# Delta rule's preparation: four buffers for the decay factors, masks in the preparation's own pool, gating weights in the weight ring, and the last triangular inverses behind the first head's loads

## The chip, the cores and the metric

The kernel runs on one core of a Trainium2 chip. The metric is the device time of one execution in microseconds (us), as the median of several runs. The names of the engines in the profile are: PE the matrix engine (PEld its weight loads), DVE the vector engine, ACT the scalar engine, POOL the general engine, SP the engine whose queue issues nearly all transfers.

## The reference, cut to what matters

The program computes a hybrid layer (a mixer of delta rule and differential attention, then experts) and after it a second block (a state space branch, sparse attention, a feed-forward part). The change lies in the mixer of the first block. Its delta rule, chunk by chunk:

```
a_mat = eye + b * (k k^T) * dec_strict          # one 64x64 triangle a chunk and head
sol   = triangular_solve(a_mat, [b*exp(G)*k, b*v])
def step(s, xs):                                # in order over the chunks, both directions
    u = ub - w @ s
    o = qd @ s + aqk @ u
    return gl * s + kd^T @ u, o
```

and its differential attention, for 4 heads and blocks of 128 queries, with 256 context tokens ahead of 1024 own keys:

```
s = einsum('bqhid,bkhid->bhiqk', qi, k)         # two maps i for each head
p = softmax(s)
a = p[:, :, 0] - lam * p[:, :, 1]
o = einsum('bhqk,bkhe->bqhe', a, v)
```

Both outputs, normed and gated, go side by side through `w_out`.

## The kernel before, in words

Everything here happens in `stage_mixer`, in chunks of 128 tokens: 10 tiles (tiles 0 and 1 are the context), 4 heads, two directions d.

First come the projections. After the convolutions of q, k and v, `gdn_prep` treats one tile: it transposes and norms k, q and v, makes k k^T (`kks`) and q k^T (`qks`), and for each direction the decays: the matmul of `g` with `tri` gives the sums of log decays in PSUM, one matmul with `mask` (L423) adds -2^60 where the triangle is empty, ACT takes exponents into a tile `e1` (shown as `e`), DVE multiplies it by `qks` (L428, stored to DRAM as `Qk`) or by `kks` (L433, stored as `Ad`). A latent tile takes four `e1` tiles: two a direction. ACT can write an `e1` only when the store that reads the buffer's last content has ended.

`gdn_invert` inverts the 32x32 diagonal blocks of `Ad` of a group of tiles, all blocks at once, a partition each: it loads them (`ia`, L452), negates into `im` (L454, L455), and goes over 31 columns with a multiply (L462) and an add (L464) on DVE, then a transposing copy (L466) and stores to `XT`. There are three groups: tiles 0 and 1; 2, 3, 8, 9; 4 to 7. The code writes each group's inverse behind the preparation of the next group; the last one stands alone, ahead of `sr.close()`.

Then follow, in the order of the code, the projections of differential attention (`da_proj_qk`), the load of head 0 (`da_load`: `dalq`, `dalk`, `da_v`, split on ACT and DVE into `da_qh`, `da_ql` L680, `da_ka` L683), and the gate projection (`gate_proj`).

The second half runs the recurrence and the attention side by side. `gdn_merge` builds the whole inverses (`mX`, `mT`) of two tiles from the 32x32 blocks (`mc<-XT`), `Ad` (`mB`) and k (`mk`); `gdn_step` makes `u` (L575), the new state `S` and outputs. There are 10 steps of two (one a direction); step 4 is the first that needs tiles of the third group. `da_unit` is one of 32 units (4 heads by 8 query blocks): six score matmul pairs (`sc`), six minima on DVE (`dst`, L713), six exponents on ACT (`E`, L714), three multiplies on POOL (L728), three combinations on DVE (L729), ten transposes (`atp`) and the product with v. Its output is `o_sb` (L744).

A scheduler fixes every engine's order when the program is built. It takes what the code writes first as more urgent, moves instructions past each other where tiles and engines are free, and so interleaves projections, preparation, recurrence and units. On the chip every engine and queue then works in its fixed order, and SP issues transfers one after the other. Pools own memory: a pool opened after another was closed may lie on the closed one's bytes, and then waits until its last reader is done. In the kernel before, `gi` (the inverse's tiles `ia`, `im`, `ix`) is closed by `sr.close()`, and the pools `hd0` and `dal` of head 0, on the right side, come behind it.

Of the kernel before, what the change touches and what calls it, by code (L numbers as in the profile page):

```python
# [10 lines left out]
F32 = mybir.dt.float32  # L11
F32R = mybir.dt.float32r
# [4 lines left out]
ALU = mybir.AluOpType  # L17
# [231 lines left out]
def gdn_scalars(K, gs, wk, ps):  # L249

    nc, I = K.nc, K.I
    sb = wk.tile([16, 4], F32, name="sb", bufs=1)
    nc.vector.memset(sb[:, 0:1], -1.0)
    nc.vector.memset(sb[0:8, 0:1], 1.0)
    nc.vector.memset(sb[:, 1:3], 0.0)
    nc.sync.dma_start(sb[0:8, 1:2], I["dt_bias"].rearrange("a d h -> (a d h)")[:, None])
    nc.sync.dma_start(sb[0:8, 2:3], I["a_log"].rearrange("a d h -> (a d h)")[:, None])
    nc.scalar.activation(sb[:, 3:4], sb[:, 2:3], AF.Exp)
    z = wk.tile([16, NT], F32, name="abz", tag="cvraw", bufs=1)
    e = wk.tile([16, NT], F32, name="abe", tag="cva")  # L260
    wr = gs.tile([128, 8, 16], F32, name="abw", bufs=1)
    nc.sync.dma_start(wr, I["w_in"][0].rearrange("(k p) n -> p k n", p=128)[:, :, 3584:3600])
    w = gs.tile([128, 8, 48], F32R, name="abh", bufs=1)
    for c in (0, 16):
        nc.scalar.activation(w[:, :, c:c + 16], wr, AF.Copy)
    nc.vector.tensor_sub(w[:, :, 32:48], wr, w[:, :, 0:16].bitcast(F32))
    for c0, n in CHUNKS:
        q = ps.tile([128, 512], F32, name="pj")
        for k in range(8):
            K.mm(q[0:48, :n], w[:, k], K.hh[:, k, c0:c0 + n], k == 0, False)  # L270
            K.mm(q[0:16, :n], w[:, k, 0:16], K.hl[:, k, c0:c0 + n], False, k == 7)
        nc.scalar.activation(e[:, c0:c0 + n], q[32:48, :n], AF.Copy)
        nc.vector.tensor_add(z[:, c0:c0 + n], q[0:16, :n], e[:, c0:c0 + n])
    nc.vector.tensor_scalar(z, z, sb[:, 0:1], sb[:, 1:2], op0=ALU.mult, op1=ALU.add)
    nc.scalar.activation(e, z, AF.Abs)
    nc.scalar.activation(e, e, AF.Exp, scale=-1.0)
    nc.scalar.activation(e, e, AF.Ln, bias=1.0)
    nc.vector.tensor_scalar(z, z, 0.0, None, op0=ALU.max)
    nc.vector.tensor_add(z, z, e)
    nc.vector.tensor_scalar(z, z, sb[:, 3:4], -1.0, op0=ALU.mult, op1=ALU.mult)  # L280
    g = gs.tile([128, 10, 16], F32, name="g_tok")
    K.g = g
    tp = K.ga.tile([128, 512], F32, name="ga")
    for t in range(10):
        nc.tensor.transpose(tp[:, t * 16:(t + 1) * 16], z[:, t * 128:(t + 1) * 128], K.ident[:16, :16])
    nc.vector.tensor_copy(g, tp[:, :160].rearrange("p (t c) -> p t c", c=16))
    K.tri = []
    for d in range(2):
        m = gs.tile([128, 128], F32, name=f"tri{d}")
        nc.gpsimd.memset(m, 1.0)  # L290
        sg = 1 if d == 0 else -1
        nc.gpsimd.affine_select(out=m, in_=m, pattern=[[sg, 128]], compare_op=ALU.is_ge, fill=0.0,
                                base=0, channel_multiplier=-sg)
        K.tri.append(m)
    cp = K.ga.tile([128, 512], F32, name="ga")
    G = cp[:, 0:80].rearrange("p (t c) -> p t c", c=8)
    for d in range(2):
        K.mm(cp[:, 40 * d:40 * d + 40], K.tri[d], g[:, :, 4 * d:4 * d + 4], True, True)
    K.mm(cp[:, 80:160], K.ones, g[:, :, 0:8], True, True)
    G = gs.tile([128, 2, 10, 4], F32, name="G")  # L300
    GL = gs.tile([128, 2, 10, 4], F32, name="GL")
    nc.vector.tensor_copy(G, cp[:, 0:80].rearrange("p (d t c) -> p d t c", d=2, c=4))
    nc.vector.tensor_copy(GL, cp[:, 80:160].rearrange("p (t d c) -> p d t c", d=2, c=4))
    K.nG = gs.tile([128, 2, 10, 4], F32, name="nG")
    nc.vector.tensor_scalar(K.nG, G, -1.0, None, op0=ALU.mult)
    K.nGb = gs.tile([128, 2, 10, 4], F32, name="nGb")
    for d in range(2):
        nc.vector.tensor_add(K.nGb[:, d], K.nG[:, d], g[:, :, 8 + 4 * d:12 + 4 * d])
    K.rq = gs.tile([128, 8, 4], F32, name="rq")
    K.identr = gs.tile([128, 128], F32R, name="identr")  # L310
    nc.vector.tensor_copy(K.identr, K.ident)
    K.mask = []
    for d in range(2):
        m = gs.tile([128, 4, 128], F32R, name=f"mask{d}")
        nc.vector.tensor_scalar(m, K.tri[d].unsqueeze(1).to_broadcast([128, 4, 128]), 2.0 ** 60, -2.0 ** 60,
                                op0=ALU.mult, op1=ALU.add)
        K.mask.append(m.rearrange("p h i -> p (h i)"))
    kds = gs.tile([128, 2, 10, 4], F32, name="kds")
    nc.vector.tensor_sub(kds, GL, G)
    nc.scalar.activation(kds, kds, AF.Exp)  # L320
    nc.scalar.activation(G, G, AF.Exp)
    nc.scalar.activation(GL, GL, AF.Exp)
    beta = gs.tile([128, 2, 10, 4], F32, name="beta")
    for d in range(2):
        nc.scalar.activation(beta[:, d], g[:, :, 8 + 4 * d:12 + 4 * d], AF.Exp)
    K.eG, K.glb, K.kds, K.beta = G, GL, kds, beta
# [41 lines left out]
def gdn_prep(K, wk, t):  # L368
    nc = K.nc
# [44 lines left out]
    for d in range(2):  # L414
        gr = K.ga.tile([128, 4, 128], F32, name="ga")
        for h in range(4):
            K.mm(gr[:, h], K.g[:, t, 4 * d + h:4 * d + h + 1].to_broadcast([128, 128]), K.tri[d], h == 0, True)
        if lat:
            eg = wk.tile([128, 4, 128], F32, name="eg", bufs=2)
            nc.scalar.activation(eg, gr, AF.Exp)  # L420
            nc.vector.tensor_mul(eg, eg, qt)
            nc.sync.dma_start(K.Qd[d, t - 2], eg)
        K.mm(gr.rearrange("p h i -> p (h i)"), K.identr, K.mask[d], False, True)  # L423
        e1 = wk.tile([128, 4, 128], F32, name="e1", bufs=2)
        if lat:
            for h in range(4):
                nc.scalar.activation(e1[:, h], gr[:, h], AF.Exp, bias=K.nG[:, d, t, h:h + 1])
            nc.vector.tensor_mul(e1, e1, qks)  # L428
            nc.sync.dma_start(K.Qk[d, t - 2], e1)
            e1 = wk.tile([128, 4, 128], F32, name="e1", bufs=2)  # L430
        for h in range(4):
            nc.scalar.activation(e1[:, h], gr[:, h], AF.Exp, bias=K.nGb[:, d, t, h:h + 1])
        nc.vector.tensor_mul(e1, e1, kks)  # L433
        nc.sync.dma_start(K.Ad[d, t].rearrange("h j i -> j h i"), e1)
# [229 lines left out]
def da_load(K, hd, lp, h):  # L664
    nc = K.nc
    q = lp.tile([128, L], F32, name="dalq")
    k = lp.tile([128, NT], F32, name="dalk")
    nc.sync.dma_start(q, K.qrd[h])
    nc.sync.dma_start(k, K.krd[h])
    v = hd.tile([128, 10, 128], F32, name="da_v")  # L670
    nc.sync.dma_start(v, K.vd[:, h * 128:(h + 1) * 128].rearrange("(t p) e -> p t e", p=128))
    lo, hi = slice(0, 64), slice(64, 128)
    Q, KA = [], []
    sub = (nc.gpsimd if h else nc.vector).tensor_sub
    for i, (a, b) in enumerate(((lo, hi), (hi, lo))):
        qh = hd.tile([128, L], F32R, name=f"da_qh{i}")
        ql = hd.tile([128, L], F32R, name=f"da_ql{i}")
        for c in (a, b):
            nc.scalar.activation(qh[c], q[a], AF.Copy, scale=-0.125)
            nc.vector.scalar_tensor_tensor(ql[c], q[a], -0.125, qh[a].bitcast(F32), op0=ALU.mult, op1=ALU.subtract)  # L680
        ka = hd.tile([128, NT], F32R, name=f"da_ka{i}")
        nc.scalar.activation(ka[a], k[a], AF.Copy)
        sub(ka[b], k[a], ka[a].bitcast(F32))  # L683
        Q.append((qh, ql))
        KA.append(ka)
    return Q, KA, v
# [106 lines left out]
def stage_mixer(K, cst, dr):  # L793

    nc, I, tc = K.nc, K.I, K.tc
# [21 lines left out]
    with ExitStack() as s0:  # L817
        gs = K.pool(s0, "gs", 1)
        sp = s0.enter_context(ExitStack())
        K.ga = K.pool(sp, "gap", GAB, PSUM)  # L820
        sr = s0.enter_context(ExitStack())
        with ExitStack() as s1:
# [6 lines left out]
            with ExitStack() as s2:  # L829
                wk = K.pool(s2, "cvw", 2)  # L830
                da_lambda(K, wk, ps)
                gdn_scalars(K, gs, wk, ps)
                w = wcols(K, win, 2048)
# [6 lines left out]
                gdn_conv(K, wk, ps, wcols(K, win, 1536), 0, K.qTd)  # L840
                gdn_conv(K, wk, ps, wcols(K, win, 2560), 2, K.vTd)
            dp = K.pool(s1, "dpw", 2)
            gi = K.pool(sr, "gi", 1)
            wk = K.pool(sr, "gw", 1, side="right")
            ahead = []
            for ts in ((0, 1), (2, 3, 8, 9), (4, 5, 6, 7)):
                for t in ts:
# [1 line left out]
                if ahead:  # L849
                    gdn_invert(K, gi, ahead.pop())  # L850
                ahead.append(ts)
            gdn_invert(K, gi, ahead.pop())
            sr.close()
            hdp = [K.pool(s0, "hd0", 1, side="right")]
            lp = K.pool(s0, "dal", 1, side="right")
# [10 lines left out]
                da_proj_qk(K, wk, ps, w, h, K.krd, True)  # L866
            w = wcols(K, win, 3072)
            hd = da_load(K, hdp[0], lp, 0)
            gate_proj(K, wk, ps, w)
        with ExitStack() as s1:  # L870
            sp.close()
# [1647 lines left out]
```

## Time and profile before

| | us |
|---|---|
| median of 3 runs | 3219.5 (3216.84 to 3223.82) |
| profiled execution, own time | 3220.71 |
| its span from first to last instruction | 3219.0 |
| its mean granted clock of PE | 0.952 of full |
| busy in the span: PE / DVE / ACT / POOL | 2899.8 / 2399.3 / 1635.2 / 654.3 |
| last projection matmul of the mixer starts | 527.41 |
| first score matmul of the first attention unit | 636.5 |
| last transfer of the mixer's outputs issued | 1042.12 |

All positions are us from the start of the profiled span. The stretch between the last three rows is where this change works; from 1042 on, the order of the program is not touched. "Busy" is the time in which at least one instruction runs on the engine, so overlapping ones are not counted twice.

### The profile page before, as it was taken

The numbers are of one execution on the slowest core, as the hardware profiler recorded it, in microseconds if no ns is written. First come the engines' busy times: TensorE is split into PE (matmuls) and PEld (weight loads), VectorE is DVE, ScalarE is ACT, GpSimd is POOL, SyncE is SP. The second block draws the span as 40 slices with busy tenths as digits, with TensorE's granted clock in tenths as the row PEclk, the third lists the DMA queues.
The fourth block names the chain that finished last, engine by engine and source line by source line (L and its number), as shares of the span: only waits on it lengthen the run. The fifth ranks groups of instructions, "written<-read, shape, count | busy, mean of one in ns | idle before, by whom it ended". The sixth has DMA issues, their size and how long they took to land.

```text
span 3219.0 us, 45364 instructions
## 1 busy us (share of the span) xinstructions
PE 2899.8 (90%) x15797; PEld 2390.6 (74%) x15797; DVE 2399.3 (75%) x4935; ACT 1635.2 (51%) x3127; POOL 654.3 (20%) x606
## 2 busy tenths in 40 slices
PE   6899996688897959999999699998798999999999
PEld 3678885677786748887777577776686788888787
DVE  4387676879887499999988599986566686555675
ACT  3333454246676228887777477663443243333343
POOL 1000111245545521110100424432225000000000
PEclk8999998789899979999999899999899999999999
DMA  6466655643224449999997223224575323333732
GB/s 224 114 209 183 192 180 169 177 118 111 71 77 140 176 181 379 384 398 373 364 367 265 84 63 92 66 64 136 147 237 183 118 72 105 111 110 100 291 112 102
DMA packets 366211, 567.04 MB, mean 176 GB/s; under 512 B 72581, under 2 KB 207646, under 8 KB 365982
## 3 DMA queue, kind: packets, MB, share of 16 engines
q1 hardware_dynamic: 361374, 547.37, 50.1%
q0 software_dynamic: 4608, 16.78, 2.2%
q8 instruction: 124, 2.03, 0.3%
q14 instruction: 105, 0.86, 0.1%
HBM read 446.12 MB, written 117.95 MB: 175 GB/s over the span
## 4 chain that ended last, share of the span: by engine, by line
PE 65%; DVE 18%; DMA 7%; issue 4%; ACT 4%; POOL 1%; SPq 1%; DVEq 0%; ACTq 0%; POOLq 0%
PE pj L57 37%; PE pu L57 5%; PE pg L57 5%; PE py L57 4%; PE ga L57 3%; PE lg L57 2%; PE atp L57 2%; DVE E L729 1%; DVE bjv L1778 1%; DVE dst L713 1%; DVE wl L1229 1%; PE sc L57 1%; DMA s5wo<-s5o 1%; DMA wmod<-in_w_mod_dram 1%; PE tp L1252 1%
## 5 line engine op out<-in xcount | busy, mean ns | idle before, releaser
L1229 DVE TENSOR_TENSOR wl<-wraw,wh 128x1024 fp32r<-128x1024 f32 x384 | 446.7, 1219 | 10.6 <-ACT wh L1228 10.3
L1228 ACT ACTIVATE wh<-wraw 128x1024 fp32r<-128x1024 f32 x384 | 391.7, 1060 | 79.6 <-PE pu L57 36.9
L57 PE MATMUL pj<-hh,wh 128*128 128x512 f32 (+1 forms) x768 | 296.7, 386 | 10.7 <-ACT uo L1928 7.7
L57 PE MATMUL pj<-hl,wh 128*128 128x512 f32 (+1 forms) x768 | 292.4, 381 | 0.0
L57 PE MATMUL pj<-hh,wl 128*128 128x512 f32 (+1 forms) x768 | 292.1, 382 | 0.0
L57 PE MATMUL pj<-wh,hh 128*128 128x512 f32 (+1 forms) x400 | 161.0, 403 | 18.7 <-DVE g L2018 8.5
L57 PEld LDWEIGHTS pj<-hh,wh 128*128 128x128 f32 x768 | 145.4, 189 | 42.4 <-ACT uo L1928 10.9
L57 PEld LDWEIGHTS pj<-hh,wl 128*128 128x128 f32 x768 | 144.8, 189 | 30.1 <-issue 3.9
L57 PEld LDWEIGHTS pj<-hl,wh 128*128 128x128 f32 x768 | 145.5, 189 | 26.9 <-issue 2.9
L57 PE MATMUL pj<-wh,hl 128*128 128x512 f32 (+1 forms) x400 | 159.2, 399 | 1.6 <-DVE hl L214 1.5
L57 PE MATMUL pj<-wl,hh 128*128 128x512 f32 (+1 forms) x400 | 159.9, 400 | 0.0
L714 ACT ACTIVATE E<-sc,dst 128x512 f32<-128x512 f32 (+1 forms) x192 | 117.4, 616 | 71.7 <-DVE dst L713 66.2
L75 ACT ACTIVATE wh<-wraw 128x1024 fp32r<-128x1024 f32 (+2 forms) x88 | 88.8, 1015 | 91.2 <-DMA wraw<-in_w_in_dram 36.6
L76 POOL TENSOR_TENSOR wl<-wraw,wh 128x1024 fp32r<-128x1024 f32 (+1 forms) x44 | 100.2, 2281 | 138.1 <-ACT wh L75 137.9
L713 DVE TENSOR_REDUCE dst<-sc 128x1 f32<-128x512 f32 (+1 forms) x192 | 108.7, 594 | 10.5 <-PE sc L57 9.4
L57 PE MATMUL pu<-wl,xh 128*128 128x512 f32 x256 | 101.6, 397 | 11.3 <-DVE wl L1229 11.0
L728 POOL TENSOR_TENSOR E<-E,dst 128x512 f32<-128x512 f32 (+1 forms) x96 | 97.5, 1044 | 65.6 <-DVE dst L725 37.2
L57 PE MATMUL sc<-da_ka,da_qh 128*128 128x512 f32 (+1 forms) x192 | 81.3, 427 | 30.8 <-ACT E L714 30.8
L1775 ACT ACTIVATE bja<-isc,bca 128x384 bf16<-128x384 f32 (+2 forms) x96 | 79.4, 827 | 51.6 <-DVE bca L1793 24.8
L57 PEld LDWEIGHTS pj<-wh,hh 128*128 128x128 f32 x400 | 77.9, 195 | 35.9 <-DVE g L2018 8.9
L1292 POOL DMA_INDIRECT xacc<-ye,ix x16 | 37.1, 2318 | 324.9 <-DVE ye L1291 239.2
L57 PE MATMUL pg<-wl,xh 128*128 128x512 f32 x256 | 102.6, 401 | 0.2 <-DVE wl L1229 0.2
(825 smaller groups left out, 8513.4 us busy)
## 6 DMA issues: line engine op xcount, KB each, us to landing
wraw<-in_w_gate_dram SPq DMA_DIRECT2D x64, 1024.0 KB
wraw<-in_w_up_dram SPq DMA_DIRECT2D x64, 1024.0 KB
wraw<-in_w_down_dram SPq DMA_DIRECT2D x64, 1024.0 KB
wraw<-in_w_in_dram SPq DMA_DIRECT2D x52, 512.0 KB
raw<-hsd SPq DMA_DIRECT2D x38, 512.0 KB
mw<-in_w_mod_dram SPq DMA_DIRECT2D x32, 512.0 KB
raw<-in_w_ffn_gate_dram SPq DMA_DIRECT2D x22, 512.0 KB
raw<-in_w_ffn_up_dram SPq DMA_DIRECT2D x22, 512.0 KB
```

The lines of the kernel that those rows point to most:

```text
L57: self.nc.tensor.matmul(out, lhsT, rhs, start=start, stop=stop, skip_group_check=True)
L75: nc.scalar.activation(h, raw, AF.Copy)
L76: self.sub(l, raw, h.bitcast(F32))
L713: nc.vector.tensor_reduce(mn[:, i, j:j + 1], p[:, :n], axis=AX.X, op=ALU.min)
L714: nc.scalar.activation(e[:, c0:c0 + n], p[:, :n], AF.Exp, bias=mn[:, i, j:j + 1], scale=-1.0, accum_out=ls[:, i, j:j + 1])
L728: nc.gpsimd.tensor_mul(e1, e1, sc[:, 1, j:j + 1].to_broadcast([128, n]))
L729: nc.vector.scalar_tensor_tensor(e0, e0, sc[:, 0, j:j + 1], e1, op0=ALU.mult, op1=ALU.add)
L1228: nc.scalar.activation(h, raw[:, k], AF.Copy)
L1229: nc.vector.tensor_sub(l, raw[:, k], h.bitcast(F32))
L1252: nc.tensor.transpose(tp[:, k], src[:, (k0 + k) * 128:(k0 + k + 1) * 128], K.ident)
L1292: nc.gpsimd.indirect_dma_start(out=K.xacc, out_offset=bass.IndirectOffsetOnAxis(ap=idx[e][:, :1], axis=0), in_=ye, in_offset=None, compute ...
L1775: self.K.nc.scalar.activation(jk[:, :self.n], self.x, AF.Sign, bias=cand, scale=-1.0, accum_out=cnt)
```

## The change: what it does

1. `e1` gets four buffers in the place of two.
2. The two `mask` tiles are no longer made in the long-lived pool `gs` but in the preparation's own pool `gw`, ahead of the first `gdn_prep`.
3. The gating weights `abw` and `abh` take slots of the weight ring's pools (`wraw`, `wh`) in the place of places of their own in `gs`.
4. `gi` is opened in the scope `s1`, which lives until the projections are through, so `sr.close()` no longer closes it.
5. The last `gdn_invert` (tiles 4 to 7) is written behind head 0's `da_load` and ahead of `gate_proj`.

```diff
--- before.py
+++ after.py
@@ -258,9 +258,9 @@
     nc.scalar.activation(sb[:, 3:4], sb[:, 2:3], AF.Exp)
     z = wk.tile([16, NT], F32, name="abz", tag="cvraw", bufs=1)
     e = wk.tile([16, NT], F32, name="abe", tag="cva")
-    wr = gs.tile([128, 8, 16], F32, name="abw", bufs=1)
+    wr = K.wraw.tile([128, 8, 16], F32, name="abw", tag="wraw")
     nc.sync.dma_start(wr, I["w_in"][0].rearrange("(k p) n -> p k n", p=128)[:, :, 3584:3600])
-    w = gs.tile([128, 8, 48], F32R, name="abh", bufs=1)
+    w = K.wh.tile([128, 8, 48], F32R, name="abh", tag="wh")
     for c in (0, 16):
         nc.scalar.activation(w[:, :, c:c + 16], wr, AF.Copy)
     nc.vector.tensor_sub(w[:, :, 32:48], wr, w[:, :, 0:16].bitcast(F32))
@@ -309,12 +309,6 @@
     K.rq = gs.tile([128, 8, 4], F32, name="rq")
     K.identr = gs.tile([128, 128], F32R, name="identr")
     nc.vector.tensor_copy(K.identr, K.ident)
-    K.mask = []
-    for d in range(2):
-        m = gs.tile([128, 4, 128], F32R, name=f"mask{d}")
-        nc.vector.tensor_scalar(m, K.tri[d].unsqueeze(1).to_broadcast([128, 4, 128]), 2.0 ** 60, -2.0 ** 60,
-                                op0=ALU.mult, op1=ALU.add)
-        K.mask.append(m.rearrange("p h i -> p (h i)"))
     kds = gs.tile([128, 2, 10, 4], F32, name="kds")
     nc.vector.tensor_sub(kds, GL, G)
     nc.scalar.activation(kds, kds, AF.Exp)
@@ -421,13 +415,13 @@
             nc.vector.tensor_mul(eg, eg, qt)
             nc.sync.dma_start(K.Qd[d, t - 2], eg)
         K.mm(gr.rearrange("p h i -> p (h i)"), K.identr, K.mask[d], False, True)
-        e1 = wk.tile([128, 4, 128], F32, name="e1", bufs=2)
+        e1 = wk.tile([128, 4, 128], F32, name="e1", bufs=4)
         if lat:
             for h in range(4):
                 nc.scalar.activation(e1[:, h], gr[:, h], AF.Exp, bias=K.nG[:, d, t, h:h + 1])
             nc.vector.tensor_mul(e1, e1, qks)
             nc.sync.dma_start(K.Qk[d, t - 2], e1)
-            e1 = wk.tile([128, 4, 128], F32, name="e1", bufs=2)
+            e1 = wk.tile([128, 4, 128], F32, name="e1", bufs=4)
         for h in range(4):
             nc.scalar.activation(e1[:, h], gr[:, h], AF.Exp, bias=K.nGb[:, d, t, h:h + 1])
         nc.vector.tensor_mul(e1, e1, kks)
@@ -840,8 +834,14 @@
                 gdn_conv(K, wk, ps, wcols(K, win, 1536), 0, K.qTd)
                 gdn_conv(K, wk, ps, wcols(K, win, 2560), 2, K.vTd)
             dp = K.pool(s1, "dpw", 2)
-            gi = K.pool(sr, "gi", 1)
+            gi = K.pool(s1, "gi", 1)
             wk = K.pool(sr, "gw", 1, side="right")
+            K.mask = []
+            for d in range(2):
+                m = wk.tile([128, 4, 128], F32R, name=f"mask{d}")
+                nc.vector.tensor_scalar(m, K.tri[d].unsqueeze(1).to_broadcast([128, 4, 128]), 2.0 ** 60, -2.0 ** 60,
+                                        op0=ALU.mult, op1=ALU.add)
+                K.mask.append(m.rearrange("p h i -> p (h i)"))
             ahead = []
             for ts in ((0, 1), (2, 3, 8, 9), (4, 5, 6, 7)):
                 for t in ts:
@@ -849,7 +849,6 @@
                 if ahead:
                     gdn_invert(K, gi, ahead.pop())
                 ahead.append(ts)
-            gdn_invert(K, gi, ahead.pop())
             sr.close()
             hdp = [K.pool(s0, "hd0", 1, side="right")]
             lp = K.pool(s0, "dal", 1, side="right")
@@ -866,6 +865,7 @@
                 da_proj_qk(K, wk, ps, w, h, K.krd, True)
             w = wcols(K, win, 3072)
             hd = da_load(K, hdp[0], lp, 0)
+            gdn_invert(K, gi, ahead.pop())
             gate_proj(K, wk, ps, w)
         with ExitStack() as s1:
             sp.close()
```

The change moves instructions on several engines. On SP (the queue of transfers), head 0's loads `dalq` and `dalk` stood behind the last inverse's stores (`XT<-ix`, `XT<-im`) and behind the reloads of `mB` for the fourth merge:

```order
L472 DMA XT<-ix 4x4x1024
L472 DMA XT<-im 4x4x1024
L472 DMA XT<-ix 4x4x1024
L498 DMA mB_5840<-Ad 128x4x128
L498 DMA mB_5841<-Ad 128x4x128
L668 DMA dalq<-qrd 128x1024
L669 DMA dalk<-krd 128x1280
```

Now they stand between the two halves of the loads of the last inverse's blocks (`ia<-Ad`), behind the reload of `mB` for the second merge; the stores of that inverse come 33 rows further down the queue:

```order
L489 DMA mc_5679<-XT 128x8x32
L604 DMA gsg<-sgd 128x512
L492 DMA mB_5498<-Ad 128x4x128
L492 DMA mB_5499<-Ad 128x4x128
L446 DMA ia<-Ad 16x32x32 x4
L662 DMA dalq<-qrd 128x1024
L663 DMA dalk<-krd 128x1280
L665 DMA da_v<-vd 128x10x128
L446 DMA ia<-Ad 16x32x32 x4
```

So head 0's loads no longer follow the last inverse, but its inputs. On PE, at the end of the preparation, the masks of the last tile (`ga<-mask`) stood ahead of the first merge (`gm<-mc,mB`):

```order
L57 MATMUL ga<-tri_941,g_tok 128x128 x4
L57 MATMUL ga<-mask_960,identr 128x512
L57 MATMUL ga<-mask_962,identr 128x512
L57 MATMUL gm<-mc_5391,mB_5387 32x32 x8
L57 MATMUL gm<-mc_5403,mB_5388 32x32 x8
```

and now the merge's first half stands ahead of them:

```order
L57 MATMUL ga<-tri_941,g_tok 128x128 x4
L57 MATMUL gm<-mc_5391,mB_5387 32x32 x8
L57 MATMUL ga<-mask_2989,identr 128x512
L57 MATMUL ga<-mask_2991,identr 128x512
L57 MATMUL gm<-mc_5403,mB_5388 32x32 x8
```

What moved is the first merge, past the last tile's masks. On DVE, the first units' minima (`dst<-sc`) stood behind the whole last inverse (its last copy is `im<-ix`), six `u` and head 0's splits; the end of that stretch was:

```order
L683 TENSOR_TENSOR da_ka_5096<-dalk,da_ka_5096 64x1280
L683 TENSOR_TENSOR da_ka_5105<-dalk,da_ka_5105 64x1280
L502 COPY mX_5377<-mc_6065 32x4x32 x4
L575 TENSOR_TENSOR u<-ga,beta 128x512
L713 TENSOR_REDUCE dst<-sc 128x1 x3
```

Now the first minima stand behind the inverse's first column, and columns and minima alternate:

```order
L677 TENSOR_TENSOR da_ka_5010<-dalk,da_ka_5010 64x1280
L458 TENSOR_TENSOR ix<-ix,ia 128x31
L497 COPY mT_5379<-mc_5844 32x4x32 x2
L707 TENSOR_REDUCE dst<-sc 128x1 x2
L456 TENSOR_TENSOR ia<-im,ix 128x30x2
L707 TENSOR_REDUCE dst<-sc 128x1
```

The last inverse moved from ahead of the attention units into them: its last copy stands behind 6 `u` and 3 finished units (`o_sb`) now, and stood behind 2 `u` and none before.

## Rows read from the trace of the kernel before

**Rows 1.** The page's section 1: busy time, share of the span, instructions.

```profile
PE 2899.8 (90%) x15797; PEld 2390.6 (74%) x15797; DVE 2399.3 (75%) x4935; ACT 1635.2 (51%) x3127; POOL 654.3 (20%) x606
```

**Rows 2.** Busy time by stretch: us, PE, PEld, DVE, ACT, POOL (instructions), clock, DMA share, GB/s.

```profile
480.00:520.00 40.00, 39.62 (x217) 33.83 (x216) 34.47 (x86) 18.79 (x67) 3.90 (x3) 1.00 0.55 180
...
561.70:608.70 47.00, 28.38 (x352) 25.79 (x352) 41.52 (x125) 6.14 (x17) 9.07 (x8) 0.58 0.56 149
608.70:636.50 27.80, 20.06 (x265) 18.45 (x265) 20.14 (x35) 10.06 (x15) 9.74 (x8) 0.94 0.74 236
636.50:680.00 43.50, 29.97 (x313) 27.30 (x312) 36.93 (x66) 21.90 (x53) 19.99 (x14) 0.80 0.41 119
680.00:960.00 280.00, 252.06 (x2209) 221.82 (x2208) 238.68 (x560) 176.10 (x548) 141.10 (x136) 0.93 0.31 94
960.00:1042.20 82.20, 63.34 (x409) 52.37 (x408) 64.31 (x149) 56.50 (x171) 47.62 (x62) 0.95 0.36 122
551.60:1042.20 490.60, 393.81 (x3540) 345.72 (x3541) 404.75 (x942) 270.70 (x804) 228.43 (x230) 0.88 0.40 117
```

**Rows 3.** Timelines of PE and ACT, 527 to 582: start, us, instruction, [idle before <-releaser].

```profile
527.41 0.39 PE L57 MATMUL pj<-wh,hl 128*128 128x512 f32 x1
...
548.72 1.14 ACT L427 ACTIVATE e<-ga,nG 128x128 f32<-128x128 f32 x4 [4.24 <-DMA Qk<-e]
...
563.82 0.84 PE L57 MATMUL gm<-mc,mB 32*32 32x32 f32 x16 [20.85 <-DMA mB<-Ad]
...
580.58 2.08 PE L57 MATMUL ga<-sv,mX 128*128 128x128 f32 x8 [1.58 <-DVE mX L540]
```

**Rows 4.** Timeline of SP's queue, 548 to 558: start, time to issue, transfer.

```profile
548.08 0.57 SPq L472 DMA_DIRECT2D XT<-ix  x1
...
552.12 0.43 SPq L434 DMA_DIRECT2D Ad<-e  x1
...
557.73 0.63 SPq L498 DMA_DIRECT2D mB<-Ad  x1
```

**Rows 5.** The chain that ended last, 607 to 638: start, us, piece.

```profile
607.67 1.04 DVE im L466
...
617.23 2.53 DMA XT<-ix
619.90 3.91 DMA dalq<-qrd
...
624.98 1.22 DVE da_ql L680
...
636.11 1.50 DVE da_ka L683
```

**Rows 6.** Timelines of DVE and of POOL around 587.

```profile
586.14 0.42 DVE L464 TENSOR_TENSOR ix<-ix,ia 128x255 f32<-128x255 f32 x1
...
587.05 1.14 DVE L464 TENSOR_TENSOR ix<-ix,ia 128x252 f32<-128x252 f32 x1
...
586.70 1.22 POOL L578 TENSOR_TENSOR kd<-mk,kds 128x512 f32<-128x512 f32 x1 [14.46 <-issue]
```

**Rows 7.** DVE's two costliest groups by form, 551.6 to 1042.2: count | busy, mean ns | idle before.

```profile
L713 DVE TENSOR_REDUCE dst<-sc 128x1 f32<-128x512 f32 x128 | 86.0, 683 | 7.5 <-PE sc L57 6.6
L729 DVE SCALAR_TENSOR_TENSOR E<-E,dst,E 128x512 f32<-128x512 f32 x64 | 66.8, 1056 | 9.2 <-POOL E L728 9.0
```

**Rows 8.** Tile views of `o_sb`, `mask` and `abh`, and the last `u` of the timeline.

```profile
L744 DVE SCALAR_TENSOR_TENSOR o_sb<-atp,oss,dagr x32: 333/344/353, 685.4 to 1040.6; 128x128 f32<-128x128 f32 x32
...
960.77 0.68 DVE L575 TENSOR_TENSOR u<-ga,beta 128x512 f32<-128x512 f32 x1
...
L315 DVE TENSOR_SCALAR mask<-tri x2: 422/422/422, 4.0 to 4.3; 128x512 fp32r<-128x512 f32 x2
...
L265 ACT ACTIVATE abh<-abw x2: 292/292/293, 38.5 to 38.7; 128x128 fp32r<-128x128 f32 x2
...
L57 PE MATMUL pj<-hh,abh x24: 387/396/449, 130.3 to 140.6; 128*48 128x512 f32 x16, 128*48 128x256 f32 x8
```

## The prediction

> **What bounds the kernel now.** I read the page's busy times first, then the busy time by stretch, and inside the mixer the timelines, the chain that ended last and the groups by form. Over the whole span PE is the engine to look at (90% busy, DVE 75%) [rows 1], but that is an average. While the projections run, PE is full: 39.62 of 40 us from 480 to 520 [rows 2], until the last projection matmul at 527.41 [rows 3]. Waits of the preparation on other engines before that moment cost nothing, because PE has projections to do meanwhile. Between 527 and the first score this changes: PE sits idle for 20.85 us until the first merge at 563.82 [rows 3], then works at a granted clock of 0.58 until 608.7 with DVE the busier engine (41.52 of 47 us), and from 608.7 to 636.5 neither is full (20.06 and 20.14 of 27.8) [rows 2]. From 680 to 960, with recurrence and attention side by side, PE has 90% and DVE 85%; at the end, 960 to 1042, 77% and 78% [rows 2].
>
> What holds the first score back is the chain: the last inverse's copy at 607.67, its stores, the last of which is issued at 617.23 and takes 2.53 us, only then head 0's load at 619.90 (3.91 us to land), then the splits until 637.61 [rows 5]. The load waits since it lies on the inverse's memory. Nothing in it needs the inverse. The first unit ends at 685.4, the thirty-second at 1040.6 [rows 8].
>
> **The change part by part.** *Masks and gating weights.* The masks cost 2 × 0.42 us on DVE wherever they are made [rows 8]; now they lie in the projections, PE full, so nothing; uncovered 0.84 us. The gating weights' cast at 38.5 is used at 130.3 [rows 8], 92 us later. Sharing the weight ring delays one prefetched weight unit by the cast and the subtraction behind it; the bound is a gain of 0 and a loss of about 1 us, and I take 0. The freed memory has no duration of its own.
>
> *Four buffers of e1.* ACT waited for the store of `Qk` before the last tile's exponents (4.24 us at 548.72 [rows 3]); earlier waits of this kind are hidden by the projections. This could let the preparation end some 4 us sooner. The new order takes part of it back: PE now has the first merge's first half ahead of the last masks, so these wait for `mB` and `mc` to land. That load's issue was at 557.73, behind the second inverse's stores, the last at 548.08, and the last tile's store at 552.12 [rows 4]; now it follows right behind the inverse's stores. I take 547 (545 to 551). From issue to matmul it took 6.1 us, so the merge starts at 553 in the place of 563.8, and 16.8 us later (563.82 to 580.58 [rows 3]) the first `u` product, at 570 in the place of 580.6. That is about 11 us on a stretch that ended in waiting, not yet a gain at the end.
>
> *Head 0's load.* Its place on SP is behind the reload of `mB` for the second merge, which waits until the first merge has read the buffer, some 13 us after its first matmul by the pace of those 16.8 (566), and behind half of the inverse's inputs, whose last store of `Ad` follows the delayed masks (exponents, product, store: about 563). So the load goes out at about 568. From its issue to the end of the splits took 17.7 us before (619.90 to 637.61 [rows 5]), so the first scores come at about 585, with 575 to 595 for the uncertain landing times, against 636.5 [rows 2]. The attention starts some 50 us sooner.
>
> *The last inverse.* It isn't cheaper: 62 steps of a column and three larger operations on DVE, about 25 us. Before it ran as the only heavy work on DVE, now it runs between the units. So not 50 us are won, only what DVE left idle. I count DVE's work along its new order, each row by the mean duration of its form in this stretch (the two costliest are shown, 683 and 1056 ns [rows 7]). From 551.6 to 1042.2 this gives 443 us in both orders (404.75 busy [rows 2], since neighbours overlap). From the first minima to the inverse's last copy the new order has 82 us: 61 inverse operations 23.7, 34 minima 20.2, 15 combinations 14.4, the recurrence's copies, `u` and `S` 16.3, small ones 7.4. With the 35 ahead of it, 117 us are then done. The order before has done 113 us at its first `o_sb`, at 685.4 [rows 8], and the other 330 in 357 us, a rate of 0.92; so it had done 117 at 689.
>
> At which rate does DVE work through the 82? Along the old order the count stands at 8 us at 561.7, 54 at 608.7, 78 at the first minima (639) and 113 at 685.4: a rate of 0.97 with the inverse filling every gap, 0.80 behind it, and 0.77 from the first minima on. With units, recurrence and inverse all at hand it is nearest to the first and to the 0.92 of the mixed stretch; I take 0.92 to 0.97. From 586 that ends at 670 to 675, 14 to 19 us ahead of 689. The rest of the work is the same for both, and I give it the same time. Sum: 16 us. Against the profiled execution's own 3220.7 that is 3204.7; the median of the runs shown lies 1.2 below that execution, so 3203.5.
>
> *A cost inside the inverse.* An inverse operation of 252 columns took 1.14 us while POOL ran `kd`, its neighbour of 255 took 0.42 [rows 6]: 0.72 us for a collision. POOL was busy 9.07 of 47 us beside the inverse before, and 19.99 of 43.5 where the units run [rows 2]. If each of the 61 is hit that much more often, 61 × (0.46 − 0.19) × 0.72 = 12 us are added. If other work of DVE is hit that much less, since POOL's work is the same in all, nothing is. I take 2 of it as inside the rate above, which is that of a stretch with such collisions.
>
> The Trainium skill, "GPSIMD Engine Reference", section "Specifications", says that POOL shares its SBUF interfaces with DVE, in contention with instructions that read two SBUF operands; every column of the inverse is one. By that rule the move is into the worse neighbourhood and the sum would be about 4 us of gain, by the row's spread over the other work 16.
>
> **The rivals.**
> - *DVE swallows it* (no change). Collisions add the 12 us, or the rate stays at the 0.77 of 639 to 685: 82 / 0.77 = 106 us, to 692 in the place of 689. For it: DVE's minima then wait for PE's scores and ACT's exponents, and an order fixed ahead makes columns wait behind minima. Against: in that stretch there was no inverse to fill. Result 3217 (3213 to 3224).
> - *The recurrence ends last* (slower). The ninth `u` is the first that needs the last inverse. By the count it comes at 675 + 60 / 0.92 = 740, before at 698. Before, the last `u` followed at 960.8 [rows 8], 262 us or 23.8 per `u`; after it 10 units came in 81 us. Now 7 units stand behind the last `u`, 57 us. If the pace stays at 23.8, because each step waits for the one before, the end is at 740 + 262 + 57 = 1059, 17 us late: 3236. It decides from 22.3 us per `u` on. For it: POOL's `kd` and `tS` and the merges stand in every step. Against: from the first product at 580.58 [rows 3] to 685.4 eight `u` came, 13 us each, so the chain alone is faster, and the new order has 224 us of DVE's work in this part where the old has 248.
> - *More than DVE's count* (much faster). The inverse's columns fill all of DVE's waits (443 / 404.75 = 1.09 is the rate of a DVE that is always busy), scores start at 575, and PE's clock, 0.58 behind its idle time [rows 2], recovers sooner: 576 + 82 / 1.09 = 651, 38 us ahead. Result 3182. Against: no stretch of the mixer shows DVE always busy.
> - *The buffers and pools do nothing.* If the load of head 0 found other memory to wait for, the end would be as before; the new order puts the load ahead of the inverse's stores, so this has little chance. It is counted with the first.
>
> **How the numbers follow.** My forecast (gain of 7 to 30) has 0.63, the first rival 0.17, the slower one 0.12, the much faster one 0.08. A change under 0.2% (6.4 us) can't be told from none in this kernel. Faster takes 0.63, 0.08 and nothing of the others, less 0.02 since my forecast's lower end lies near the bound; same 0.18, slower 0.13. The forecast alone spans 3189 to 3213. For 8 in 10 the range reaches up into the first rival and down into the last: 3186 to 3224.
>
> **What would show it.** Right: first `sc` at 575 to 595 with `dalq` issued ahead of the inverse's stores; the inverse's last copy at about 670 with three `o_sb` before it; the first `o_sb` near 640; the last transfer of the mixer at 1020 to 1030, the stages behind unmoved in length. Step by step wrong: PE's idle time ahead of the first merge still 20 us (then SP's queue, not the wait for e1, set it); inverse operations mostly at 1.1 us (collisions); `u` paced over 22 us from the ninth on (recurrence). The prediction as a whole fails if the first scores come early and the end doesn't move, or if time shows up ahead of 527 or behind 1042.

## The result, and the profile after

The changed kernel takes 3206.0 us (median of 5 runs, 3201.0 to 3208.5) beside 3223.7 us before in the same comparison (5 runs): ratio 0.9943, 95% interval 0.9931 to 0.9955, 17.7 us faster. The prediction had 3203.5 us and 16 us of gain. The profiled execution has a span of 3199.2 us and took 3200.96.

The mixer's last unit ends 19 us sooner, and what follows the mixer is as long as it was (2178.4 us from the last `o_sb` to the end of the span before, 2177.4 now). The text ahead of the prediction has it that the order there is untouched. It is not quite: SP's queue, for one, issued a load of expert weights at 1114.69 and then a store of `xacc` at 1115.94, and now issues the store first (1094.13, 1096.50). The tile view of `o_sb` in the changed kernel (first and last start at the end of the numbers), which answers to [rows 8]:

```profile
L738 DVE SCALAR_TENSOR_TENSOR o_sb<-atp,oss,dagr x32: 335/344/352, 624.7 to 1021.8; 128x128 f32<-128x128 f32 x32
```

The first unit moved from 685.4 to 624.7, the last only from 1040.6 to 1021.8: of 61 us won at the front, 19 are left at the end.

PE's timeline of the changed kernel around the first merge and the first score, which answers to [rows 3]:

```profile
549.35 0.74 PE L57 MATMUL gm<-mc,mB 32*32 32x32 f32 x16 [3.65 <-DMA mB<-Ad]
550.02 1.22 PE L57 MATMUL ga<-mask,identr 128*128 128x512 f32 x2
...
566.06 2.08 PE L57 MATMUL ga<-sv,mX 128*128 128x128 f32 x8 [0.51 <-DVE mX L534]
...
584.58 0.80 PE L57 MATMUL sc<-da_ka,da_qh 128*128 128x512 f32 x1 [3.31 <-DVE da_ka L677]
```

(Lines are left out at the dots, here and below.) The 20.85 us of idle PE ahead of the first merge are 3.65 us now, the last tile's masks stand behind its first half as the order said, and the first score comes 52 us sooner. On SP's queue (start, time to issue) head 0's load stands where the order had it, behind the reloads of `mB` and the first inputs of the inverse; this answers to [rows 4, 5]:

```profile
565.17 0.94 SPq L492 DMA_DIRECT2D mB<-Ad  x2
566.16 2.38 SPq L446 DMA_DIRECT2D ia<-Ad  x4
568.58 0.48 SPq L662 DMA_DIRECT2D dalq<-qrd  x1
```

By stretch (us, PE, PEld, DVE, ACT, POOL, clock, DMA share, GB/s), which answers to [rows 2]:

```profile
561.70:608.70 47.00, 34.86 (x328) 30.64 (x329) 37.53 (x93) 19.77 (x45) 9.44 (x9) 0.62 0.65 161
608.70:636.50 27.80, 25.74 (x252) 23.20 (x247) 25.20 (x65) 13.94 (x42) 12.32 (x14) 0.88 0.20 58
636.50:680.00 43.50, 39.06 (x392) 35.07 (x390) 42.67 (x102) 25.71 (x72) 20.48 (x22) 1.00 0.39 120
680.00:960.00 280.00, 240.39 (x2177) 211.49 (x2173) 239.79 (x544) 168.60 (x519) 140.93 (x132) 0.91 0.36 105
960.00:1023.30 63.30, 48.32 (x312) 40.52 (x313) 51.01 (x110) 40.86 (x122) 36.35 (x52) 0.95 0.41 135
551.60:1023.30 471.70, 391.92 (x3524) 344.09 (x3525) 405.90 (x939) 273.60 (x818) 221.60 (x227) 0.88 0.40 119
```

DVE's whole work is the same (405.90 beside 404.75 us). It is denser in 608.7 to 680 (67.87 of 71.3 us, before 57.07), and PE with it (64.80, before 50.03). In 680 to 960 PE has less work than before in as many us (240.39, before 252.06), at a granted clock of 0.91 (before 0.93): that is where part of PE's lead goes. DVE's lead stays (239.79, before 238.68).

### The profile page after: what moved, and what is told of

The parts are those of the page before. It is cut to its first block, busy times and chain, and to the rows that moved or that the text cites. A ratio compares the mean times of both kernels' runs of the same rounds, so it can differ in the third digit from the quotient of the medians.

```text
span 3199.2 us, 45340 instructions
## 1 busy us (share of the span) xinstructions
PE 2898.8 (91%) x15797; PEld 2389.5 (75%) x15797; DVE 2396.0 (75%) x4935; ACT 1634.3 (51%) x3127; POOL 661.9 (21%) x606
## 4 chain that ended last, share of the span: by engine, by line
PE 65%; DVE 18%; DMA 7%; issue 4%; ACT 3%; POOL 2%; SPq 1%; DVEq 0%; ACTq 0%; POOLq 0%
PE pj L57 38%; PE py L57 5%; PE pu L57 5%; PE pg L57 5%; PE ga L57 2%; PE lg L57 2%; DVE dst L707 2%; DMA s5wo<-s5o 1%; DVE E L723 1%; DVE bjv L1778 1%; DMA wmod<-in_w_mod_dram 1%; PE sc L57 1%; PE tp L1252 1%; PE gm L57 1%; DVE tw L1101 1%
## 5 line engine op out<-in xcount | busy, mean ns | idle before, releaser
L1292 POOL DMA_INDIRECT xacc<-ye,ix x16 | 49.9, 3121 | 318.7 <-DVE ye L1291 238.0
```

Source lines behind the costliest of these rows:

```text
L1292: nc.gpsimd.indirect_dma_start(out=K.xacc, out_offset=bass.IndirectOffsetOnAxis(ap=idx[e][:, :1], axis=0), in_=ye, in_offset=None, compute ...
```

## The experiments

Each row is one kernel, the profile's first score and the first and last `o_sb`, what is left of the span behind the last `o_sb`, the median and the ratio to the kernel before, run on the same chip, with its 95% interval. The positions are of one profiled execution each.

| kernel | first `sc` | `o_sb` first, last | behind it | median us | ratio |
|---|---|---|---|---|---|
| before | 636.5 | 685.4, 1040.6 | 2178.4 | 3222.7 to 3224.9 | 1 |
| changed | 584.6 | 624.7, 1021.8 | 2177.4 | 3206.0 | 0.9943 (0.9931 to 0.9955) |
| e1 weights in the ring only | 574.5 | 618.3, 1008.0 | 2184.5 | 3191.8 | 0.9900 (0.9887 to 0.9914) |
| e2 change without parts 4, 5 | 586.6 | 623.6, 1018.7 | 2190.9 | 3210.2 | 0.9959 (0.9945 to 0.9972) |
| e3 change with two `e1` | 569.3 | 615.1, 1020.7 | 2181.7 | 3203.8 | 0.9935 (0.9922 to 0.9949) |
| e4 change, no columns | 585.2 | 634.3, 1014.8 | 2183.7 | 3202.0 | 0.9933 (0.9916 to 0.9950) |
| e5 e1 and 2 KB taken back | 635.3 | 679.9, 1034.5 | 2180.3 | 3223.6 | 0.9999 (0.9990 to 1.0009) |
| e6 e1 and four `e1` | 586.6 | 623.0, 1018.3 | 2186.8 | 3206.3 | 0.9933 (0.9915 to 0.9950) |
| e7 parts 2 and 3 | 575.0 | 618.3, 1012.7 | 2183.5 | 3198.0 | 0.9920 (0.9905 to 0.9934) |
| e8 before, no columns | 589.6 | 640.0, 1023.8 | 2183.3 | 3212.2 | 0.9965 (0.9951 to 0.9978) |
| e9 e1, five units a step | 571.7 | 615.1, 1009.7 | 2193.6 | 3203.7 | 0.9939 (0.9926 to 0.9953) |
| e10 e6, five units a step | 589.2 | 626.0, 1027.9 | 2187.8 | 3218.3 | 0.9983 (0.9974 to 0.9992) |
| e11 e1, units written later | 572.0 | 616.0, 1011.3 | 2187.3 | 3200.4 | 0.9927 (0.9913 to 0.9940) |

The last two columns hold more than the mixer. The stages behind it are in no edit, but the scheduler can order them anew when the mixer changes: e11 changes one number of e1's mixer, and on SP's queue some 900 us behind it two rows have changed places (first e1, then e11):

```profile
1928.98 0.41 SPq L72 DMA_DIRECT2D wraw<-in_w_in_dram  x1
1929.67 0.35 SPq L1862 DMA_DIRECT2D aqt<-qsd  x1
```

```profile
1931.34 0.33 SPq L1862 DMA_DIRECT2D aqt<-qsd  x1
1931.71 0.43 SPq L72 DMA_DIRECT2D wraw<-in_w_in_dram  x1
```

The length behind the last `o_sb` goes from 2177.4 to 2193.6 us between these executions. So a difference of some 10 us between two medians is not yet one of the mixer; for that the last `o_sb` is the better witness, to about 5 us (see e7).

The theory was that head 0's load was held by memory and nothing else ("room"); the rivals, that the preparation's four buffers or the new place of the inverse did it.

**e1, the weights alone.** To the kernel before, part 3 only:

```diff
-    wr = gs.tile([128, 8, 16], F32, name="abw", bufs=1)
+    wr = K.wraw.tile([128, 8, 16], F32, name="abw", tag="wraw")
...
-    w = gs.tile([128, 8, 48], F32R, name="abh", bufs=1)
+    w = K.wh.tile([128, 8, 48], F32R, name="abh", tag="wh")
```

> The kernel before with part 3 of the change alone: the gating weights in the weight ring, 2 KB a partition less in the long-lived pool; two e1 buffers, masks, inverse's pool and its place as before. Theory 'room': what counts is that head 0's load no longer lies on the inverse's memory, and 2 KB are enough for that (the load had 7.9 KB left and needs 9). In this order the load stands ahead of the last inverse's stores; the first scores come before 600 us and the time falls by 14 to 20 us against before, as with the whole change. Rival 'preparation': the gain comes from e1's four buffers and the earlier first merge; then this kernel gains 0 to 6 us. Rival 'place of the inverse': the gain needs the inverse written behind the load; then it is 0 to 8 us.

It gained 33 us, nearly twice what the whole change does. Those two lines free 2 KB a partition and touch nothing near the attention. On SP's queue of this kernel head 0's load goes out at 560.25, ahead of the first merge's `mB`:

```profile
558.04 2.16 SPq L452 DMA_DIRECT2D ia<-Ad  x4
560.25 1.06 SPq L668 DMA_DIRECT2D dalq<-qrd  x1
...
562.32 0.99 SPq L498 DMA_DIRECT2D mB<-Ad  x1
```

The price is paid by the recurrence (the first merge's matmuls, PE's timeline of the same kernel) and not at the end:

```profile
569.37 0.87 PE L57 MATMUL gm<-mc,mB 32*32 32x32 f32 x16 [23.43 <-DMA mB<-Ad]
...
574.46 0.79 PE L57 MATMUL sc<-da_ka,da_qh 128*128 128x512 f32 x1
```

PE waits for `mB` even longer than in the kernel before ([rows 3]: 20.85), and the kernel is the fastest of all. Shortening that wait is not what gains.

**e5, the 2 KB taken back.** To e1:

```diff
         gs = K.pool(s0, "gs", 1)
+        pad = gs.tile([128, 512], F32, name="pad", bufs=1)
+        nc.gpsimd.memset(pad, 0.0)
```

> The kernel of e1 (gating weights in the ring) with an unused tile of 2 KB a partition in the long-lived pool, so that head 0's pool lies on the inverse's memory again. Theory 'room': the load stands behind the last inverse's stores again (it does in the order), first scores near 636 us, the time is that of the kernel before within 6 us (3218 to 3231). Rival 'weights': the gain of e1 comes from the weight ring at the start or from the order that goes with it; then 10 us or more of its 33 us are left.

Ratio 0.9999, first score back at 635.3, and the load behind the last inverse's stores again:

```profile
616.21 0.58 SPq L472 DMA_DIRECT2D XT<-ix  x1
616.90 0.95 SPq L498 DMA_DIRECT2D mB<-Ad  x2
618.86 0.33 SPq L668 DMA_DIRECT2D dalq<-qrd  x1
```

With e1 this shows the cause: whether head 0's pool `dal` lies on the inverse's memory. The addresses that the program is built with say the same. In the kernel before and in e5 `ix` ends at byte 189536 of a partition and `dalq` begins at 188384; in e1 `ix` ends at 187488, so that 896 bytes lie between them. The weight ring itself is worth nothing that shows in the time; the last `o_sb` of e5 comes 6 us ahead of that of the kernel before.

**e2, without parts 4 and 5.** To the changed kernel:

```diff
-            gi = K.pool(s1, "gi", 1)
+            gi = K.pool(sr, "gi", 1)
...
+            gdn_invert(K, gi, ahead.pop())
             sr.close()
...
             hd = da_load(K, hdp[0], lp, 0)
-            gdn_invert(K, gi, ahead.pop())
```

> The change without its parts 4 and 5: the inverse's pool closes with the preparation, and the last inverse is written ahead of head 0's load, as before; four e1 buffers, masks and weights as in the change. Theory 'room': the load still has memory of its own, first scores at 580 to 595 us, last inverse's copy a few us sooner than in the change (the count of DVE's rows up to it is 109 us in the place of 117), time within 5 us of the change, so 13 to 22 us below before. Rival 'place of the inverse': the inverse runs ahead of the units again, first scores behind 600 us, and at most half of the gain is left (0 to 9 us).

First score at 586.6, last `o_sb` at 1018.7, median 4 us above the changed kernel with intervals that overlap. So the load is free without the pool's scope and the inverse's place, and beside four `e1` buffers these are worth nothing that shows. Part 4 could not have freed it alone either: with `gi` kept open in the kernel before, 7.9 KB are left for `dal`, which needs 9.

**e3 and e6, two and four `e1`.** e3 is the changed kernel with `bufs=2` in both `e1` lines, e6 is e1 with `bufs=4`.

> The change with two e1 buffers in the place of four. Theory 'room': the wait for the store of Qk returns in the last tiles (4 to 5 us each), the first merge and u come some 10 to 20 us later, but scores come no later than in the change, so the time is 0 to 6 us above the change. Rival 'preparation': most of the gain is lost, the time lies 10 us or more above the change.

> The kernel of e1 with four e1 buffers in the place of two and nothing else. Theory 'four buffers cost': with them the scheduler puts the first merge ahead of the last masks, the loads and scores come some 10 us later (585 in the place of 575), and the mixer ends 8 to 14 us later than in e1, 3200 to 3206. Rival 'chance of the order': the loss against e1 comes from anything that reshuffles the rows; then this lies anywhere between 3190 and 3210, with its loss not in the first scores. If four buffers help as meant, it is 3186 to 3192.

In the changed kernel the two extra buffers make no difference that shows (0.9935 without, 0.9943 with), though without them the first scores come 15 us sooner. On e1 they cost 14 us by the medians (one of e6's six runs took 3191.8, as e1 does) and 10 at the last `o_sb`, as the theory had it. SP's queue of e6 shows the way: the load stands behind the second merge's `mB` and all eight inputs of the inverse:

```profile
566.23 0.93 SPq L498 DMA_DIRECT2D mB<-Ad  x2
567.21 6.24 SPq L452 DMA_DIRECT2D ia<-Ad  x8
573.50 0.48 SPq L668 DMA_DIRECT2D dalq<-qrd  x1
```

13 us later than in e1.

**e7, masks and weights.** Parts 2 and 3 of the change with two `e1` buffers, `gi` and the inverse as before.

> Parts 2 and 3 of the change: masks in the preparation's own pool and weights in the ring; two e1 buffers, the inverse's pool and its place as before. Its rows of DVE up to the inverse's end are those of e1. Theory 'the place of the inverse costs': against the run with two e1 buffers and the inverse written behind the load (3203.8) it is 8 to 14 us faster, 3190 to 3196, like e1. Rival 'the masks' place costs': it is at 3200 to 3206, and e1 was faster through its masks.

3198.0 lies between the two ranges: 6 us from e3 and 6 from e1, and the intervals of neighbours overlap. The traces say more. Up to the 24th unit e7 runs as e1 does (24th `o_sb` at 936.8, in e1 at 936.1); its last unit comes 4.7 us later, in a stretch with a granted clock of 0.91 beside 0.93, so a difference of that size is no sign of the edit. e3 differs from e7 by parts 4 and 5, and its last unit comes at 1020.7, 8 us behind e7's, though its first scores come 6 us sooner. So with two `e1` buffers the inverse's new place seems to cost at the last unit, by little more than that scatter. e2 against e7 has four buffers cost 6 us there, and 12 by the medians.

**e4 and e8, the inverse's columns left out.** In the changed kernel and in the one before:

```diff
-    for j in range(31, 0, -1):
+    for j in range(31, 0 if ts[0] != 4 else 30, -1):
```

> The change with 30 of the 31 columns of the last inverse left out (the matrices of tiles 4 to 7 are then not inverted); stores and loads stay. It takes away 22 to 24 us of DVE's work between the units. Theory 'DVE bounds this stretch': the end moves by that work over the rate of 0.92, 22 to 28 us below the change. Rival 'the inverse fills waits': the columns lie in time that DVE would wait, and the end moves by less than 10 us.

> The kernel before with 30 of the 31 columns of the last inverse left out (tiles 4 to 7 are then not inverted). Here the head's load waits for the inverse. Theory 'the inverse was on the path': the first scores move up by the columns' 24 us and by more where the order lets them, and the time falls by 20 to 40 us to 3185 to 3204, where the same cut in the changed kernel gave 4 us. Rival 'DVE's work': the cut gives the same few us in both.

Both theories about DVE missed, and e4's rival (less than 10 us) has its number; e8's (the same few us in both) has not. The changed kernel gained 4 us, which its interval does not tell from none (7 at the last `o_sb`), the one before 12 (17 at the last `o_sb`), where 22 to 28 and 20 to 40 were expected. In e8 head 0's load goes out at 576.26, the first scores come 47 us sooner than in the kernel before, and DVE has less work, yet it gains less than half of what e1 does: a first score that comes sooner does not set the end by itself. By stretch, from 640 to 680, first the changed kernel and then e4:

```profile
640.00:680.00 40.00, 35.56 (x337) 31.73 (x336) 39.17 (x94) 23.30 (x64) 19.13 (x20) 1.00 0.39 120
```

```profile
640.00:680.00 40.00, 38.89 (x418) 35.61 (x417) 34.68 (x87) 22.72 (x71) 21.33 (x23) 1.00 0.33 94
```

With the columns DVE is full (39.17 of 40), without them PE nearly is (38.89). PE did 3.3 us more in this stretch. The cut also changed the order (the first `o_sb` comes 10 us later than with the columns, at 634.3), so e4 prices the columns together with another order, and not alone.

**e9, e10, e11, the units' place in the code.** e9 and e10 set `DAU` to 5 in e1 and e6, e11 sets `DA0` to 6 in e1 (before `DAU, DA0 = 4, 3`).

> The kernel of e1 with five attention units written behind each step of the recurrence in the place of four (DAU 5). The order up to the last inverse's end is that of e1; behind the last u there are 25 us of DVE's work in the place of 40. Theory 'tail': units alone, behind the recurrence, leave PE and DVE at some 80%, so a shorter tail gains 2 to 6 us against e1, 3186 to 3190. Rival 'recurrence last': its outputs then end the mixer, and the time is 3194 or more.

> The kernel of e6 (weights in the ring, four e1 buffers) with five units behind each step. Behind the last u the order has 32 us of DVE's work in the place of 59. Theory 'tail': four buffers cost because the recurrence starts sooner and ends sooner, and the units are left alone longer; then this takes back most of the 14 us, 3192 to 3199, with first scores still at 585. Rival 'late scores': four buffers cost because the first scores come 12 us later; then it stays at 3201 to 3208.

> The kernel of e1 with the attention units written three steps of the recurrence later (DA0 6 in the place of 3); the order up to the last inverse's end is that of e1, behind it rows change place. Five units a step cost 12 us with two and with four e1 buffers. Theory 'recurrence first in the mixed part': the later the units are written, the sooner the recurrence is through, and the time is at or below that of e1, 3186 to 3193. Rival 'chance of the order': e1's order is a lucky one, and this one lies at 3196 to 3206 as well.

The theory of the tail fell: with a shorter tail both kernels are 12 us slower. "Late scores" has not won by that, since e10 (3218.3) lies above its range too. e9's rival has its number (3194 or more) but not its way: its last `u` starts at 980.3, 29 us ahead of its last `o_sb`. And e11 lies where "chance of the order" had it.

But the medians mix two things. In the mixer e9 and e11 end as e1 does to within 4 us (last `o_sb` at 1009.7 and 1011.3, in e1 at 1008.0), and the rest of their 12 and 9 us lies behind it or in other executions than the profiled one. By the last unit the kernels whose load is free fall into two groups. With two buffers and the inverse where it was (e1, e7, e9, e11) it comes at 1008.0 to 1012.7; with four buffers, with the inverse moved, or with both, at 1014.8 to 1027.9 (the 1014.8 is e4, which has the columns left out). Four buffers cost 10, 6 and 18 us there, from e1 to e6, e7 to e2 and e9 to e10, and the moved inverse 8 (e7 to e3); the smaller of these are little above the scatter of 5, but all have one sign. Both together cost no more than the one (e3 to the changed kernel: 1 us). One view goes with these groups: ACT's exponents waiting for DVE's minima, 665 to 960 (total us, times, longest), first in the changed kernel and then in e1:

```profile
ACT E L708 <- DVE dst L707: 52.1, 35, 7.0
```

```profile
ACT E L714 <- DVE dst L713: 36.1, 28, 2.6
```

The total is 30.6 to 39.3 us in the first group (e7 36.2, e9 39.3, e11 30.6) and 52.1 to 60.6 in the second (e2 59.1, e3 56.4, e4 60.6, e6 57.4, e10 59.2). That is read, not tested: which rows of the fixed order make those waits, and whether the waits are what puts the last unit off, stays open.

## Why the prediction was right, and where it was not

**The steps up to the first score held to within 4 us.** `mB` out at 547: 545.56 and 547.52. First merge at 553: 549.35. First `u` product at 570: 566.06. Load at 568: 568.58. First scores at 585: 584.58. They were read from one place in SP's order and from delays of the kernel before, and the queue gives them. A little of it is luck: the merge started 4 us sooner than forecast, and the reload of `mB` behind it, at 565.17, came 16 us after it and not 13.

**The sum came out near, by two errors that cancel.** DVE's 82 us from the first minima to the inverse's last copy were to take 85 to 89 us at a rate of 0.92 to 0.97. The copy starts at 664.20 and the first minimum at 588.3: 77 us, a rate of 1.07, so the lead there is 24 us and not 14 to 19. That is near the 1.09 which the prediction gave to a DVE that is always busy and kept for its fastest rival. (The 0.77 from the first minima on is 0.75 by the prediction's own counts, 35 us in 46.4; only the first rival uses it.) Then "the rest of the work is the same for both, and I give it the same time" failed: of the 24 us 5 are given back by the last `o_sb`. The 680 to 960 row above has PE at 86% where it was 90%.

**Collisions were seen, and they were a small cost.** The two lines of the inverse's columns, first before (561 to 609), then in the changed kernel (574 to 666), count | busy, mean ns:

```profile
L464 DVE TENSOR_TENSOR ix<-ix,ia 128x31 f32<-128x31 f32 (+15 forms) x31 | 12.2, 393 | 1.0
L462 DVE TENSOR_TENSOR ia<-im,ix 128x31 f32<-128x31 f32 (+15 forms) x31 | 11.4, 366 | 1.1
```

```profile
L456 DVE TENSOR_TENSOR ia<-im,ix 128x31 f32<-128x31 f32 (+15 forms) x31 | 15.7, 506 | 0.2
L458 DVE TENSOR_TENSOR ix<-ix,ia 128x31 f32<-128x31 f32 (+15 forms) x31 | 13.3, 428 | 0.3
```

23.6 us became 29.0, 5.4 more, between the 0 and 12 of the prediction. The same form twice in the changed kernel, alone and beside a multiply of POOL, and that multiply:

```profile
585.19 0.22 DVE L456 TENSOR_TENSOR ia<-im,ix 128x31 f32<-128x31 f32 x1
...
662.92 1.02 DVE L456 TENSOR_TENSOR ia<-im,ix 128x31 f32<-128x31 f32 x1
```

```profile
662.55 1.34 POOL L541 TENSOR_TENSOR bk<-mk,G 128x512 f32<-128x512 f32 x1 [0.82 <-PE gm L57]
```

What this is worth at the end no run separates; e4, without nearly all of the columns, ends its last unit 7 us sooner. The Trainium skill, "GPSIMD Engine Reference", section "Specifications", names this contention between POOL and DVE instructions with two SBUF operands; the trace agrees that it is there (0.22 and 1.02 us above), and not that it brings the gain down to 4 us, since 17.7 were measured.

**"The freed memory has no duration of its own" was the step that failed in the reasons.** The prediction set the masks and the weights at 0 us and read the free load off the new order, without asking which part of the change makes that order. e1, e5 and e2 show which: 2 KB of freed memory free the load (33 us, and with a pad none), and parts 4 and 5, which move the inverse, are not needed for it. The time was right since all parts stand in one kernel, and that is luck as far as the reasons go: 33 us that the prediction did not see, less the 14 or so that the buffers and the inverse's place take away, which it did not see either.

**"Four buffers of e1" was taken as a small help that the new order partly takes back.** Alone on top of e1 they cost 14 us by the medians and 10 at the last unit. The prediction saw the first merge ahead of the last masks and took its 11 us as a step forward; in e1, which lacks it, the first merge starts 20 us later than in the changed kernel (569.37, 549.35), and the kernel ends sooner.

**"DVE left idle" was the wrong model of the gain.** It says that the inverse costs its 25 us of DVE wherever it stands. Left out it gave 4 and 12 us (e4, e8), as far as kernels in another order can tell.

**The rivals.** "Recurrence ends last" came close to its condition: the ninth `u` at 726.20, the last at 972.68, 22.4 us each, where 22.3 was the point. It did not decide, since the first scores' lead had brought the ninth 14 us sooner than the count had it, and the units behind the last `u` took 49 us and not 57. "DVE swallows it" and the much faster case did not happen in the changed kernel; e1 shows that 33 us were there.

**The faster version.** e1, two lines of the change and none of the rest, takes 3191.8 us: 33 us below the kernel before, and some 14 below the changed one.

## What to carry to other kernels

Where pools decide who waits, read which pool lies on which before reading which instruction stands ahead of which: a few kilobytes in an unrelated pool can hold a whole stage, and a pad of that size is the experiment that proves it. Then try each part of a change alone, since a part that looks like help (more buffers, an earlier start) can move a fixed order so that a more important transfer comes later. Read the end of the stage that was edited beside the whole time, because the order of later stages can move with it. A row with one engine full is no price list: leave the work out and see what the next engine allows, and look whether the order stayed the same.

## What was not expected of the hardware

DVE sat at 39.17 of 40 us and could lose some 24 us of its work with 7 us of effect at the last unit and none in the time that is clear of noise; PE rose from 35.56 to 38.89 of the same 40. An add on 31 columns took 1.02 us beside a multiply of POOL and 0.22 alone, and yet over the 62 operations that came to 5.4 us. And moving the units' place in the mixer (e11) ended the mixer 3 us later and the program 9, with rows of SP's queue changed some 900 us behind it.
